# Constants for a hybrid GLA and RWKV-7 step: made on ScalarE at the start instead of on VectorE, with the planner's numbers set anew

## The chip, the cores and the metric

One core of one Trainium2 chip runs the kernel. The metric is the device time of one execution in microseconds (us). The engines are TensorE (PE in the profile; its weight loads are PEld), VectorE (DVE), ScalarE (ACT), GpSimd (POOL) and SyncE (SP), which issues all transfers.

## The reference

One layer of a decoder that has two parallel branches and a gated merge, for 1024 prompt tokens (they start from zero states) and 8 sample tokens (each with its own states). Everything is float32, the model is 1024 wide.

```python
p = x @ w_in                                    # 1024 -> 9360 columns
p_gla, p_rwkv, p_gate = split(p)
q, k, v, g_a, a_lr = split(p_gla)               # a_lr: 16 columns
log_a = log_sigmoid(a_lr @ gla_alpha_w2 + b) / 16
o_gla, S_gla = gla_chunked(q, k, v, log_a, S0)  # S_t = diag(a_t) S + k_t^T v_t ; o_t = q_t S_t
o_gla = rmsnorm(o_gla) * silu(g_a)
pr = p_rwkv + (prev - p_rwkv) * mu              # token shift
r, kb, vb, g_b, w_lr, aa_lr = split(pr)
...
y, S_rwkv = rwkv7_scan(r, w, k, v, kk, a, S0)   # S_t = S (diag(w) - kk^T (kk*a)) + v^T k ; y_t = S_t r_t
o_rwkv = (groupnorm(y) + bonus) * silu(g_b)
m = sigmoid(gate_a) * (o_gla @ w_up_gla) + sigmoid(gate_b) * (o_rwkv @ w_up_rwkv)
y_out = layernorm(2**0.25 * x + m @ w_out)
```

The outputs are `y_out` for both groups, the new states and the last projected row.

## The kernel before

Every large product is made of three TensorE passes on float32r parts: a value is split into a high part `hi` (a cast) and a low part `lo` (value minus high part), and `w_hi x_hi + w_hi x_lo + w_lo x_hi` is summed in PSUM. So ahead of the products stand, for each 128x520 block of x, a cast on ScalarE (`xh<-row`) and a subtraction on VectorE or GpSimd (`xl<-row,xh`), and for each 128x512 piece of weight a cast on ScalarE (`wpart<-wraw`) and a subtraction (`wpart<-wraw,wpart`). x lies in eight blocks of 128 rows (k = 0 to 7). The tokens go through in two passes: the first holds 512 prompt tokens and the 8 samples (tiles of 256 and 264 columns), the second 512 prompt tokens (one tile of 512).

The work is written as generators ("streams": blocks of the projection, GLA heads, pairs of RWKV heads, loads, gates). `Order.run` is a list scheduler that runs while the kernel is built. At each step it asks every stream for its next operation, estimates when that could start (`start`, from `self.time` of each engine, the time at which each tile is ready, and a table of hops between engines, `HOP`, with an extra `SPARE` where TensorE takes something from ScalarE, VectorE or GpSimd), subtracts the stream's precedence (`PRIO`, or `FOR_PE` for TensorE) and emits the best. The streams give the order on each engine; no engine leaves the order that was emitted. So a change of a number in these tables, or of any operation, can deal the whole order anew. `URGENT` is subtracted for the loads of weights and x while TensorE has no weight ready (`needed`). `SPARE_ROWS` and `EARLY_GATES` say how many row buffers stay free, and how many gates are loaded early, in `load_gates`.

What the start needs: `first_blocks` runs the first two blocks of the projection over the blocks of x as they arrive, with idle products (`pch<-warm`) between. `low_rank` makes the 16 columns of `a_lr` as a product of its own. Its weights stand in the constant `wa`, 66 columns wide for each k with the high part in columns 0 to 15, the low part in columns 32 to 47 and zeros between; its result goes into `alr`, of which rows 0 to 15, 32 to 47 and 64 to 79 are written and the others must be zero. `onesr` is a 128x128 matrix of ones. These three are float32r, and are written as copies of a float32 row: in `load_constants` VectorE sets a row to one, copies it into `onesr`, sets it to zero, and copies it into `alr` and `wa`. `load_constants` runs as a stream, so the scheduler places these five operations. `setup`, ahead of the scheduler, sets the tiles `XT` (two), `Yd` and `Xd` to zero on GpSimd.

In a GLA head (`gla_head`) each chunk of 128 tokens makes, in one PSUM bank, the output `po` (from the values and, but for the first chunk, from the state `S`), and the state's increment `pS` (in a trace `big<-row` 128x256). ScalarE copies `po` out in two pieces (`row<-big` 128x128), VectorE forms the next state (`S<-S,row,big`), and the next chunk's products (`big<-row,S`) take it. In the RWKV chain TensorE works through `pch` banks: `pch<-wide,gg`, `pch<-rh,XT` and `pch<-wide`, with a copy on ScalarE or a product on VectorE after each.

Of the kernel before, what the change touches and what calls it, by code (L numbers as in the profile page):

```python
# [14 lines left out]
AF = mybir.ActivationFunctionType  # L15
# [5 lines left out]
P = 128  # L21
D = 1024
NK = D // P
# [6 lines left out]
GH, GDK, GDV = 4, 128, 256  # L30
# [15 lines left out]
HALF = HT + NS  # L46
# [18 lines left out]
GROUP = 3  # L65
IDLE = 3
RANKW, RANKM = 48, 66
SPARE_ROWS = 11
EARLY_GATES = 13


HOP = {"P": 0.2, "D": 0.418, "G": 0.115, "V": 0.064, "A": 0.14}

SWITCH = 0.092
HOLD = 0.11
TABLE = 1.28

AGE = 1.045

SPARE = 0.411  # L80
LANDED = 0.648
BIAS = 0.193
ASIDE = 8.388

PRIO = {"evacuate": 0.39, "pair": 0.3, "turn": 0.5, "chain": 0.42, "norm": 0.1, "x": 0.61, "lora": 0.42, "rank":
        1.25, "head": 0.27, "gate": -0.38, "w": 0.3, "out": 0.04, "state": -0.13, "block": -0.38}
FOR_PE = {"pair": 1.0, "turn": 1.84, "chain": 0.8, "norm": 0.39, "lora": 0.29, "rank": 1.85, "head": 0.89, "gate":
        1.0, "state": 2.11, "out": 0.05}
STAND, SCARCE, PER_ROW = 0.034, 0.249, 0.148

URGENT = 1.707
SIGMOID, EXP = "sigmoid_and_others", "natural_log_exp_and_others"
SETS = {AF.Sigmoid: SIGMOID, AF.Tanh: SIGMOID, AF.Exp: EXP, AF.Ln: EXP}

# [165 lines left out]
class Order:  # L260
# [120 lines left out]
    def run(self):  # L381
        while self.streams:
# [48 lines left out]
class Kern(Order):  # L431
# [71 lines left out]
    def setup(self):  # L503
        nc, a = self.nc, self.a
# [18 lines left out]
        for k in range(NK):  # L523
            for v in "hl":
                tag = f"x{v}{k}"
# [47 lines left out]
        for tag, n, bufs in (("XT", 2 * HT, 2), ("Yd", HT, 1), ("Xd", HT, 1)):  # L573
            ts = [cp.tile([P, n], F32, name=f"{tag}{i}") for i in range(bufs)]
            for t in ts:
                nc.gpsimd.memset(t, 0.0)
            self.fixed(tag, ts)

    def load(self, name, op):

        if name in self.first:
            yield lambda: self.first[0] == name
        yield op
        if name in self.first:
            self.first.remove(name)

    def load_constants(self):
        a, V, E = self.a, self.V, self.E
        row, wa = yield from self.rows(2)
        wa = wa[:, :NK * 16]  # L590
        yield from self.load("pv", self.S.dma_start(self.pv, a["pv"]))
        yield from self.load("wa", self.S.dma_start(wa, a["wa"]))
        yield V.memset(row, 1.0)
        yield V.tensor_copy(self.onesr, row[:, :P])
        yield V.memset(row, 0.0)
        yield V.tensor_copy(self.alr, row[0:96])
        self.has.add("alr")
        yield V.tensor_copy(self.wa, row[:, :NK * RANKW + RANKM - RANKW])
        hi, lo = (self.wa[:, :NK * RANKW].rearrange("p (k c) -> p k c", c=RANKW)[:, :, o:o + 16] for o in (0, 32))
        wa3 = wa.rearrange("p (k c) -> p k c", c=16)  # L600
        yield V.tensor_copy(hi, wa3)
        yield V.tensor_sub(lo, wa3, hi.bitcast(F32))
        self.free(wa)
        self.has.add("wa")
        yield from self.load("shift", self.S.dma_start(self.shT, a["shiftT"]))
        o = PV["mu"][0]
        yield V.tensor_scalar(self.omu, self.pv[:, o:o + NRC], -1.0, 1.0, ALU.mult, ALU.add)
        o = PV["ka"][0]
        yield V.tensor_scalar(self.oka, self.pv[:, o:o + 8], -1.0, 1.0, ALU.mult, ALU.add)
        o = PV["kk"][0]  # L610
        yield V.tensor_scalar(self.nkk, self.pv[:, o:o + 8], -1.0, None, ALU.mult)
        self.has.add("pv")
        yield from self.load("cst", self.S.dma_start(self.cons, a["cst"]))
        raw, heads = row[0:96, :GH * GDK], (yield from self.row(P))
        yield self.S.dma_start(heads, a["heads"])
        for n in range(3):
            yield self.S.dma_start(raw[32 * n:32 * n + 16], a["gla_alpha_w2"])
        yield self.S.dma_start(self.lev, a["lev"])
        yield V.tensor_copy(self.gw2, raw)
        yield V.tensor_sub(self.gw2[64:96], raw[64:96], self.gw2[64:96].bitcast(F32))  # L620
        yield V.tensor_copy(self.headsr, heads)
        self.free(row, heads)
        self.has.add("cst")
# [176 lines left out]
    def low_rank(self, c, xs):  # L800

        yield lambda: len(xs) == NK and "wa" in self.has
        x_ = yield from self.row(c.n)
        for t0, n in c.tiles:
            q = yield from self.bank("big", [P, n])
            for k in range(NK):
                for v in range(2):
                    yield self.P.matmul(q[:RANKM], self.wa[:, RANKW * k:RANKW * k + RANKM], xs[k][v][:, t0:t0 + n],
                                        start=(k == v == 0), stop=(k == NK - 1 and v == 1))
            x = x_[0:16, t0:t0 + n]  # L810
            yield self.C.copy(x, q[0:16])
            yield self.V.tensor_add(x, x, q[32:48])
            self.free(q)

            hi, lo, hi2 = (self.alr[g:g + 16, t0:t0 + n] for g in (0, 32, 64))

            yield lambda: "alr" in self.has and (not c.i or self.decayed == GH)
            yield self.C.copy(hi, x)
            yield self.C.copy(hi2, x)
            yield self.V.tensor_sub(lo, x, hi.bitcast(F32))  # L820
            c.alr_ready += 1
        self.free(x_)
# [719 lines left out]
    def load_gates(self):  # L1542

        yield lambda: self.ctx[1].fronts >= NPAIR - 1
        for n in range(2):
            for c in self.ctx:
                for x in range(NK):
                    if x == EARLY_GATES:
                        yield lambda: self.ctx[1].fronts == NPAIR and self.ctx[1].gated == NPAIR + 2 * GH
                    gt = yield from self.row(c.n, SPARE_ROWS)  # L1550
                    yield self.S.dma_start(gt, self.sg[c.i][n][x])
                    m = None
                    if n:
                        m = yield from self.row(c.n, SPARE_ROWS)
                        yield lambda: c.half > x
# [302 lines left out]
```

## Time and profile before

| | |
|---|---|
| median of three runs | 1459.84 us (1459.55 to 1460.57) |
| the profiled execution's own time | 1459.23 us |
| its span, first to last instruction | 1457.3 us |
| TensorE busy | 1443.5 us, 99% of the span |
| VectorE, ScalarE, GpSimd busy | 1058.8, 828.9, 362.6 us |
| TensorE's granted clock, mean | 0.998 |

The profile shows one execution. The time of 1459.23 us lies 1.93 us above its span, and 0.61 us under the median of the runs. A row of a timeline gives the start in us from the span's start, the time it took, engine, line, operation, output and inputs, and in brackets how long the engine had been idle and what ended that. Nearly all rows have line 227, since the helper that records operations for the scheduler stands there, so rows are told apart by the names of their tiles.

### The profile page before, as it was taken

To read this page: it belongs to the slowest core of one execution; us is meant where nothing else is said; L and a number is where in the kernel's file an instruction comes from. 1 tells how busy PE (TensorE), PEld (TensorE's weight loads), DVE (VectorE), ACT (ScalarE), POOL (GpSimd) and SP (SyncE) were. 2 spreads that over 40 slices of the span, in tenths; PEclk is the share of its full clock that TensorE was granted. 3 is DMA by queue.
4 is the path that set the end of the run, shared out by engine and by line. 5 is a ranking of instruction groups with operands and counts; after the bars stand their busy time and mean duration, and the time that the engine had idled before them with its cause. 6 is when DMAs were issued, how large, how long until landed. Compare 5 with 4: busy or idle time off the path is not lost.

```text
span 1457.3 us, 30477 instructions
## 1 busy us (share of the span) xinstructions
PE 1443.5 (99%) x10768; PEld 1280.5 (88%) x10768; DVE 1058.8 (73%) x2208; ACT 828.9 (57%) x2114; POOL 362.6 (25%) x1111
## 2 busy tenths in 40 slices
PE   9999999999999999999999999999999999999997
PEld 8999999999999998878888888888788898898786
DVE  6687487958895889577747895787669856665665
ACT  5656667766776677455555565464557646643210
POOL 1060506050604160406051405411332330000000
PEclk9999999999999999999999999999999999999999
DMA  8786887678767885675466455746575768798432
GB/s 308 262 289 201 287 275 269 202 245 297 253 209 241 277 307 191 190 210 186 137 205 208 152 173 175 229 138 207 185 230 156 226 206 249 250 311 287 135 119 84
DMA packets 211315, 319.14 MB, mean 219 GB/s; under 512 B 91699, under 2 KB 107196, under 8 KB 211164
## 3 DMA queue, kind: packets, MB, share of 16 engines
q1 hardware_dynamic: 211164, 317.20, 67.6%
q8 instruction: 86, 1.41, 0.4%
q14 instruction: 65, 0.53, 0.1%
HBM read 197.45 MB, written 118.61 MB: 217 GB/s over the span
## 4 chain that ended last, share of the span: by engine, by line
PE 92%; DVE 3%; DMA 3%; ACT 1%; issue 1%; SPq 1%; DVEq 0%; ACTq 0%
PE proj L227 59%; PE big L227 27%; PE pch L227 6%; DVE row L227 1%; SPq L227 1%; DVE xl L227 0%; DMA wraw<-w_in 0%; DMA wide<-LD 0%; DVE wpart L227 0%; DMA row<-xT 0%; DMA wraw<-w_up_gla 0%; DMA row<-o_gla 0%; DMA wide<-Sp 0%; DVE XT L227 0%; DMA w<-wpart 0%
## 5 line engine op out<-in xcount | busy, mean ns | idle before, releaser
L227 PE MATMUL proj<-xh,wpart 128*128 128x264 f32 (+2 forms) x3696 | 901.3, 328 | 0.0
L227 PEld LDWEIGHTS proj<-xh,wpart 128*128 128x128 f32 x3696 | 614.2, 188 | 49.0 <-issue 6.5
L227 PE MATMUL proj<-xl,wpart 128*128 128x264 f32 (+2 forms) x1848 | 603.8, 327 | 0.0
L227 PEld LDWEIGHTS proj<-xl,wpart 128*128 128x128 f32 x1848 | 348.1, 188 | 23.6 <-issue 1.4
L227 POOL TENSOR_TENSOR Xt<-X,wide 128x60 f32<-128x60 f32 (+24 forms) x496 | 170.9, 344 | 676.5 <-DMA wide<-LD 281.4
L227 DVE TENSOR_TENSOR row<-row 128x256 f32<-128x256 f32 (+10 forms) x369 | 191.1, 530 | 14.6 <-ACT row L227 8.0
L227 DVE TENSOR_TENSOR wpart<-wraw,wpart 128x512 fp32r<-128x512 f32 x210 | 146.1, 698 | 74.4 <-ACT wpart L227 71.2
L227 ACT CAST wpart<-wraw 128x512 fp32r<-128x512 f32 x210 | 130.0, 621 | 100.1 <-PE proj L227 57.6
L227 POOL TENSOR_TENSOR X<-X,Xt 128x60 f32<-128x60 f32 (+24 forms) x496 | 170.3, 343 | 38.7
L227 ACT ACTIVATE row<-row 128x520 f32<-128x520 f32 (+4 forms) x229 | 137.7, 612 | 13.3 <-DMA row<-sg 5.6
L227 PE MATMUL big<-xh,wpart 128*128 128x256 f32 (+2 forms) x576 | 133.0, 320 | 0.2 <-DVE wpart L227 0.2
L227 PEld LDWEIGHTS big<-xh,wpart 128*128 128x128 f32 x576 | 95.3, 188 | 7.4 <-DVE wpart L227 0.4
L227 DVE TENSOR_TENSOR wide<-pch,gg 64x65 f32<-64x65 f32 x224 | 49.8, 222 | 65.1 <-PE pch L227 62.9
L227 ACT COPY row<-big 128x128 f32<-128x128 f32 (+6 forms) x152 | 49.7, 356 | 81.1 <-PE big L227 77.0
L227 PE MATMUL big<-xl,wpart 128*128 128x256 f32 (+2 forms) x288 | 92.2, 320 | 0.8 <-DVE xl L227 0.8
L227 DVE SCALAR_TENSOR_TENSOR row<-proj,pv,row 128x255 f32<-128x255 f32 (+1 forms) x95 | 54.6, 575 | 48.2 <-ACT tail L227 36.4
L227 ACT COPY rh<-pch 128x130 f32<-128x130 f32 x121 | 32.5, 268 | 98.8 <-PE pch L227 98.0
L227 ACT COPY wide<-pch 64x65 f32<-64x65 f32 x241 | 50.1, 208 | 50.4 <-PE pch L227 47.4
L227 ACT ACTIVATE row<-proj,omu 128x256 f32<-128x256 f32 (+1 forms) x95 | 52.2, 549 | 33.5 <-PE proj L227 32.5
L409 ACT ACT_TABLE_LOAD x54 | 69.3, 1283 | 0.9
L227 PE MATMUL big<-row 128*64 128x64 f32 (+4 forms) x648 | 65.0, 272 | 0.2 <-DVE gg L227 0.2
L227 PEld LDWEIGHTS big<-xl,wpart 128*128 128x128 f32 x288 | 54.2, 188 | 5.3 <-DVE xl L227 1.8
(234 smaller groups left out, 2069.6 us busy)
## 6 DMA issues: line engine op xcount, KB each, us to landing
w<-wpart SPq DMA_DIRECT2D x146, 512.0 KB, 4.3
wpart<-w SPq DMA_DIRECT2D x146, 512.0 KB, 3.8
wraw<-w_in SPq DMA_DIRECT2D x146, 256.0 KB, 4.2
wide<-LD SPq DMA_DIRECT2D x64, 128.0 KB, 3.8
wraw<-w_up_gla SPq DMA_DIRECT2D x32, 256.0 KB, 3.7
wraw<-w_up_rwkv SPq DMA_DIRECT2D x32, 256.0 KB, 3.7
sg<-row SPq DMA_DIRECT2D x16, 260.0 KB, 3.2
row<-sg SPq DMA_DIRECT2D x16, 260.0 KB, 4.3
```

Of the source, the lines that this page charges most:

```text
L227: ways.append((eng, lambda call=call: call(out, *args, **kw), price(eng, name, out, args, ins)))
L409: self.nc.scalar.preload_act_table_set(self.table)
```

## The change

The two copies into `wa` and `alr` and the ones of `onesr` move out of `load_constants` into `setup`: ScalarE makes them from the first `XT` tile, which GpSimd has just set to zero, ahead of everything that the scheduler emits (`onesr` as the zeros plus a bias of one). The scheduler then starts with ScalarE taken to 1.9 us and GpSimd to 2.1 us. VectorE loses five operations. A memset of the row that takes the low-rank weights of the heads (`raw`) stays, and goes to GpSimd. `low_rank` no longer waits for `alr`. The planner's numbers are changed in eleven places; the order is dealt anew from them.

```diff
-SPARE_ROWS = 11
-EARLY_GATES = 13
-HOP = {"P": 0.2, "D": 0.418, "G": 0.115, "V": 0.064, "A": 0.14}
-SWITCH = 0.092
+SPARE_ROWS = 12
+EARLY_GATES = 14
+HOP = {"P": 0.2, "D": 0.385, "G": 0.115, "V": 0.064, "A": 0.14}
+SWITCH = 0.114
...
-SPARE = 0.411
+SPARE = 0.232
...  # PRIO: "gate" -0.38 -> -0.04, "out" 0.04 -> -0.08; FOR_PE: "gate" 1.0 -> 0.91
-URGENT = 1.707
+URGENT = 2.228
...
             for t in ts:
                 nc.gpsimd.memset(t, 0.0)
+            if tag == "XT":
+                zero = ts[0]
+                nc.scalar.copy(self.wa, zero[:, :NK * RANKW + RANKM - RANKW])
+                nc.scalar.copy(self.alr, zero[0:96, :HALF])
+                nc.scalar.activation(self.onesr, zero[:, :P], AF.Identity, bias=self.bias["one"])
             self.fixed(tag, ts)
+        self.time["A"], self.time["G"] = 1.9, 2.1
...
-        yield V.memset(row, 1.0)
-        yield V.tensor_copy(self.onesr, row[:, :P])
-        yield V.memset(row, 0.0)
-        yield V.tensor_copy(self.alr, row[0:96])
-        self.has.add("alr")
-        yield V.tensor_copy(self.wa, row[:, :NK * RANKW + RANKM - RANKW])
...
         yield from self.load("cst", self.S.dma_start(self.cons, a["cst"]))
+        yield self.G.memset(row, 0.0)
...
-            yield lambda: "alr" in self.has and (not c.i or self.decayed == GH)
+            yield lambda: (not c.i or self.decayed == GH)
```

What it does to the order shows at three places. The first is VectorE at the start; the names `xl` and `xh` carry the number of their buffer, and `xl_264` before is `xl_268` now (k = 4). Before:

```order
L227 TENSOR_TENSOR xl_264<-row,xh_252 128x520
L227 MEMSET row 128x520
L227 TENSOR_TENSOR wpart<-wraw,wpart 128x512
L227 CAST onesr<-row 128x128
L227 MEMSET row 128x520
L227 TENSOR_TENSOR xl_299<-row,xh_263 128x520
L227 TENSOR_TENSOR xl_314<-row,xh_298 128x520
L227 TENSOR_TENSOR xl_324<-row,xh_313 128x520
L227 CAST alr<-row 96x520
L227 CAST wa<-row 128x402
L227 CAST wa<-row 128x8x16
L227 TENSOR_TENSOR wpart<-wraw,wpart 128x512
```

And now:

```order
L227 TENSOR_TENSOR xl_268<-row,xh_256 128x520
L227 TENSOR_TENSOR wpart<-wraw,wpart 128x512 x2
L227 TENSOR_TENSOR xl_303<-row,xh_267 128x520
L227 TENSOR_TENSOR xl_319<-row,xh_302 128x520
L227 TENSOR_TENSOR xl_332<-row,xh_318 128x520
L227 CAST wa<-row 128x8x16
L227 TENSOR_TENSOR wa<-row,wa 128x8x16
```

Five operations are gone between `xl` of k = 4 and the weights of `wa`, and the second weight subtraction, which stood behind `wa`, stands ahead of `xl` of k = 5.

The second is TensorE at the same place: k = 4 of the first two blocks, and the first product with `wa`. Before:

```order
L227 MATMUL big<-xh_252,wpart 128x264
L227 MATMUL big<-xh_252,wpart 128x256
L227 MATMUL big<-xl_264,wpart 128x256
L227 MATMUL big<-xh_200,wa 66x256
L227 MATMUL big<-xl_205,wa 66x256
```

And now:

```order
L227 MATMUL big<-xl_268,wpart 128x256
L227 MATMUL big<-xh_256,wpart 128x256
L227 MATMUL big<-xh_256,wpart 128x264
L227 MATMUL big<-xl_268,wpart 128x264
L227 MATMUL big<-xh_256,wpart 128x264
L227 MATMUL big<-xh_267,wpart 128x256
L227 MATMUL big<-xl_303,wpart 128x256
L227 MATMUL big<-xh_267,wpart 128x256
L227 MATMUL big<-xh_267,wpart 128x264
L227 MATMUL big<-xl_303,wpart 128x264
L227 MATMUL big<-xh_267,wpart 128x264
L227 MATMUL big<-xh_203,wa 66x256
```

The product with `wa` has moved behind ten more products, the rest of k = 4 and half of k = 5.

The third is the state of a GLA head in the first pass, on TensorE: the increment `pS` (128x256), and the next products that take the state formed from it. Before (`S_4694` is formed from bank `big_4666`):

```order
L227 MATMUL big_4666<-row_3423 128x256
L227 MATMUL pch_4661<-wide_2683,gg_2685 128x130
L227 MATMUL proj_4592<-xl6_314,wpart_4406 128x256
L227 MATMUL proj_4592<-xh6_298,wpart_4406 128x256
L227 MATMUL proj_4592<-xh7_313,wpart_4406 128x256
L227 MATMUL proj_4592<-xl7_324,wpart_4406 128x256
L227 MATMUL proj_4592<-xh7_313,wpart_4406 128x256
L227 MATMUL big_4696<-row_3424,row_3425 128x128
L227 MATMUL proj_4692<-xh0_200,wpart_4387 128x264
L227 MATMUL big_4696<-row_2610,S_4694 128x128
```

And now, in a chunk at about the same place of the program (`S_4543` is formed from `big_4514`):

```order
L227 MATMUL big_4514<-row_3382 128x256
L227 MATMUL pch_4524<-rh_4519,XT0_179 128x130
L227 MATMUL proj_4478<-xh4_256,wpart_4223 128x264
L227 MATMUL proj_4478<-xh5_267,wpart_4223 128x264
L227 MATMUL proj_4478<-xl5_303,wpart_4223 128x264
L227 MATMUL big_4545<-row_3383,row_3384 128x128
L227 MATMUL proj_4478<-xh5_267,wpart_4223 128x264
L227 MATMUL big_4545<-row_2713,S_4543 128x128
```

Between increment and use stand eight products before and six now. On ScalarE the two copies out of that bank, which VectorE's step waits for, and what stands between them, before:

```order
L227 COPY row_2870<-big_4666 128x128
L227 COPY rh_4683<-pch_4661 128x130
L227 ACTIVATE gg_2685<-wide_2683,pc_3031 128x130
L227 COPY row_2968<-big_4666 128x128
L227 ACTIVATE row_4591<-proj_4592,omu_89 128x256
```

And now:

```order
L227 COPY rh_4519<-pch_4498 128x130
L227 ACTIVATE gg_2617<-wide_2615,pc_2875 128x130
L227 COPY row_2898<-big_4514 128x128
L227 COPY wide_2615<-pch_4524 64x65 x2
L227 COPY row_2988<-big_4514 128x128
```

Two operations stand between the copies in both; `rh` and `gg` have moved ahead, two small copies out of `pch` have come in between. Over the whole program, of the 28 steps from an increment to the next use of the state, those with eight products or fewer between are three before (eight, seven and six of them) and six now (eight, eight, six, six, five and four).

More of the change, by code (lines that the diff above doesn't have):

```diff
@@ L85 @@
 PRIO = {"evacuate": 0.39, "pair": 0.3, "turn": 0.5, "chain": 0.42, "norm": 0.1, "x": 0.61, "lora": 0.42, "rank":
-        1.25, "head": 0.27, "gate": -0.38, "w": 0.3, "out": 0.04, "state": -0.13, "block": -0.38}
+        1.25, "head": 0.27, "gate": -0.04, "w": 0.3, "out": -0.08, "state": -0.13, "block": -0.38}
 FOR_PE = {"pair": 1.0, "turn": 1.84, "chain": 0.8, "norm": 0.39, "lora": 0.29, "rank": 1.85, "head": 0.89, "gate":
-        1.0, "state": 2.11, "out": 0.05}
+        0.91, "state": 2.11, "out": 0.05}
 STAND, SCARCE, PER_ROW = 0.034, 0.249, 0.148
-URGENT = 1.707
+URGENT = 2.228
 SIGMOID, EXP = "sigmoid_and_others", "natural_log_exp_and_others"
```

## The prediction

> **What bounds the kernel now.** I read the page first (busy time and the chain that ended last), then TensorE's waits, then the start by timelines, then the one place of the waits that the new order touches most.
>
> ```profile
> PE 1443.5 (99%) x10768; PEld 1280.5 (88%) x10768; DVE 1058.8 (73%) x2208; ACT 828.9 (57%) x2114; POOL 362.6 (25%) x1111
> PE 92%; DVE 3%; DMA 3%; ACT 1%; issue 1%; SPq 1%; DVEq 0%; ACTq 0%
> ```
>
> TensorE is busy in 1443.5 of the 1457.3 us of the span, and 92% of the chain is its work. The number of products does not change. So the time can only move through what TensorE stands idle, 13.8 us in all. The stretch after the last product is a part of that:
>
> ```profile
> 1449.80:1457.30 7.50, 0.00 (x0) 0.00 (x0) 4.38 (x9) 0.50 (x2) 0.00 (x0) 0.66 0.20 70
> ```
>
> The first number after a stretch is its length, then TensorE's busy time. The last 7.5 us hold no product, only the last layer norm and its store; the change does not touch it. That leaves 6.3 us, and the view of TensorE's waits names nearly all of it:
>
> ```profile
> PE big L227 <- DVE wa L227: 1.4, 1, 1.4
> PE pch L532 <- DVE warm L529: 1.1, 1, 1.1
> PE big L227 <- DVE gg L227: 0.9, 3, 0.3
> PE big L227 <- DVE xl L227: 0.8, 3, 0.4
> PE big L227 <- DVE S L227: 0.8, 2, 0.4
> PE big L227 <- DMA wraw<-w_up_gla: 0.4, 1, 0.4
> PE pch L227 <- DMA wide<-Sp: 0.4, 1, 0.4
> ```
>
> The columns are us in total, times, and the longest. The wait for `wa` is the longest single one; the warm-up (1.1) stays in any order. All others together are 3.8 us (0.2 each for `row` and `wpart` are left out here). 0.2% of the time, about what a measurement can tell from no change, is 2.9 us: more than the wait for `wa` and less than all that can be won.
>
> **The change part by part.** *The wait for `wa`.* TensorE's rows around it, and VectorE's:
>
> ```profile
> 13.78 0.41 PE L227 MATMUL big<-xh,wpart 128*128 128x264 f32 x2
> 14.02 0.28 PE L227 MATMUL big<-xl,wpart 128*128 128x256 f32 x1
> 15.71 0.33 PE L227 MATMUL big<-xh,wa 128*66 128x256 f32 x1 [1.41 <-DVE wa L227]
> 10.37 0.49 DVE L227 MEMSET row<- 128x520 f32 x1
> 10.78 0.63 DVE L227 TENSOR_TENSOR wpart<-wraw,wpart 128x512 fp32r<-128x512 f32 x1
> 11.33 0.21 DVE L227 CAST onesr<-row 128x128 fp32r<-128x128 f32 x1
> 11.72 0.49 DVE L227 MEMSET row<- 128x520 f32 x1 [0.17 <-DVE onesr L227]
> 12.12 1.85 DVE L227 TENSOR_TENSOR xl<-row,xh 128x520 fp32r<-128x520 f32 x3
> 13.89 0.42 DVE L227 CAST alr<-row 96x520 fp32r<-96x520 f32 x1
> 14.23 0.62 DVE L227 CAST wa<-row 128x402 fp32r<-128x402 f32 x2
> 14.77 0.68 DVE L227 TENSOR_TENSOR wpart<-wraw,wpart 128x512 fp32r<-128x512 f32 x1
> 15.37 0.28 DVE L227 TENSOR_TENSOR wa<-row,wa 128x128 fp32r<-128x128 f32 x1
> 9.75 1.29 ACT L227 CAST wpart<-wraw 128x512 fp32r<-128x512 f32 x2 [0.16 <-DMA wraw<-w_in]
> 11.10 2.01 ACT L227 CAST xh<-row 128x520 fp32r<-128x520 f32 x3
> ```
>
> TensorE starts one of these products every 0.12 us (13.78, then two products on, 14.02), and the one with `wa` starts 1.69 us after the one before it: 1.57 us lost. In the new order VectorE is free by 10.37. The two weight pieces are cast by 11.04, so both subtractions (0.68 each) end by 11.75; the three `xl` follow the casts of `xh`, the last of which ends at 13.11, and end by 13.8 at the latest (0.69 after). `wa` then takes the smaller of its two casts and the subtraction of 0.28, under 0.6 us together: ready by 14.4. TensorE has ten more products ahead of it, so it gets there at 14.02 + 11 x 0.12 = 15.34. Those ten find their weights (11.75) and `xl` of k = 5 (12.5). The margin is 0.9 us, and the 1.57 us go whole. What is late next is the second tile of the same product, which waits for the first one's sum to leave its bank; it waits 0.2 now and I leave it so.
>
> *The three operations on ScalarE.* Its start, and that of the first products:
>
> ```profile
> 0.74 1.28 ACT L527 ACT_TABLE_LOAD   x1 [0.74 <-PEq L1850]
> 3.56 0.63 ACT L227 CAST xh<-row 128x520 fp32r<-128x520 f32 x1 [1.53 <-DMA row<-xT]
> 6.07 0.62 ACT L227 CAST xh<-row 128x520 fp32r<-128x520 f32 x1 [1.27 <-DMA row<-xT]
> 7.48 0.39 PE L227 MATMUL big<-xl,wpart 128*128 128x256 f32 x1 [0.35 <-DVE xl L227]
> L576 POOL MEMSET XT<- x2: 952/952/952, 0.7 to 1.6; 128x1024 f32 x2
> ```
>
> ScalarE sits idle from 2.02 to 3.56, and `XT` is zero at 0.74 + 0.95 = 1.69. A cast of 520 columns takes 0.63 and one of 512 takes 0.62 (4.18 in the same row of casts above is 0.62 after 3.56), so `alr` costs 0.63, `wa` (402 columns) some 0.5, and `onesr` (128 columns, a form not in the trace) between 0.2, VectorE's cast of that size, and 0.5. From 2.02 that ends at 3.35 to 3.68: the first `xh` is late by at most 0.12. That is hidden: the second `xh` waits for its transfer until 6.07, and TensorE waits for what comes of it at 7.48, so a start 0.12 later only shortens that wait of 0.35. Cost nothing; with the cover gone it would be 0.12.
>
> The Trainium skill (ScalarE: Activation LUTs, What ACT_TABLE_LOAD costs) gives 186 ns plus 0.833 ns a column, 93 more with a bias from memory, and an overlap of 93 between neighbours: by it an estimate of 1.34 us for the three, which would end at 3.36; the casts here (0.63 for 520) agree with its 0.62. The Trainium skill (Perfetto Trace Analysis, Optimizing Scalar/DVE Operations) speaks against such a move, since VectorE is faster where it has a performance mode: the 0.42 for `alr` on VectorE against 0.63 on ScalarE bears that out, and by it the sum would lose up to 0.2 us an operation, if ScalarE were not idle there.
>
> *GpSimd's memset of the row for the low-rank weights* stands behind the memsets of the start and is used by transfers that go out after 16 us; it costs nothing, and if it did, the wait would be for the decay of the first head, tens of us later.
>
> *The new numbers.* `SPARE` falls from 0.411 to 0.232 us: the scheduler believes that TensorE can take a result 0.18 us sooner, and puts its products that much closer behind the work that feeds them. Where the old order left a margin this costs nothing, where it had none it is a stall. The GLA state is where I can price it:
>
> ```profile
> 297.81 0.59 PE L227 MATMUL big<-row 128*128 128x256 f32 x2
> 298.24 0.39 PE L227 MATMUL pch<-wide,gg 128*128 128x130 f32 x2
> 298.44 0.27 ACT L227 COPY row<-big 128x128 f32<-128x128 f32 x1 [0.86 <-PE big L227]
> 298.66 0.27 ACT L227 COPY rh<-pch 128x130 f32<-128x130 f32 x1
> 298.82 0.41 ACT L227 ACTIVATE gg<-wide,pc 128x130 f32<-128x130 f32 x1
> 299.13 0.26 ACT L227 COPY row<-big 128x128 f32<-128x128 f32 x1
> 299.42 0.48 DVE L227 SCALAR_TENSOR_TENSOR S<-S,row,big 128x256 f32<-128x256 f32 x1 [1.06 <-ACT row L227]
> 299.95 0.50 PE L227 MATMUL big<-row,S 128*128 128x128 f32 x2 [0.40 <-DVE S L227]
> L227 ACT COPY wide<-pch 64x65 f32<-64x65 f32 x241 | 50.1, 208 | 50.4 <-PE pch L227 47.4
> ```
>
> The increment leaves TensorE at 298.40. VectorE's step waits for the second copy on ScalarE, held up by `rh` and `gg` between, and TensorE starts again at 299.95, 1.55 us after the increment and 0.40 late. In the new order two small copies (0.21 each by the last row, a group of the page) stand between instead: copies at 0.04, 0.22, 0.34 and 0.5 after the increment, its end at 0.75, VectorE 0.78 to 1.26, TensorE at about 1.3. But TensorE gets there sooner: the chain product (0.22), three products (0.36), 0.22 and 0.12 from 298.24 on would be 0.76 after the increment. So it stalls for 0.5 us, and at the other three tight places (six, five and four products between) for 0.4 to 0.5: 4 x 0.5 = 2.0 against the 0.8 of now, so 1.2 us more. From below it is 0 (ScalarE finishes sooner than I think), from above 4 x 0.9 - 0.8 = 2.8, if a delay like that of 298.66 to 299.13 comes in as well.
>
> All other waits (3.0 us without the state) are dealt anew; I take them as they are, between 0 and twice that.
>
> The sum: -1.57 + 1.2 = -0.4 against the profiled execution's 1459.23, which gives 1458.9, and 1459.5 against the median of the runs, which lies 0.6 above that execution. I say **1459.4**.
>
> **The rivals.** *Faster.* The tight places cost nothing, since ScalarE and VectorE come in time, and the other waits fall by half in an order that was dealt with more urgency for loads: -1.57 - 0.4 - 1.5 = -3.5, that is 1456.0, halfway between the two ways of counting as in the sum. For it: 5.1 us of TensorE's idle time are open to any order, and most hand-overs cost nothing even now. Against it: nothing in the diff aims at `gg`, `xl` or the two transfers in the list of waits.
>
> *Slower: the margin of 0.18 us was needed.* The rows of the RWKV chain say how much hangs on it:
>
> ```profile
> L227 PE MATMUL pch<-wide,gg 128*128 128x130 f32 x256 | 50.1, 277 | 0.4 <-DMA wide<-Sp 0.4
> L227 PE MATMUL pch<-wide 128*128 128x130 f32 x256 | 49.7, 276 | 0.0
> ```
>
> The last columns are the count, the time, and the idle time ahead. Each product is two rows, so with the one with `rh` that stands between these two the chain has 3 x 128 = 384 hand-overs, and next to no idle time ahead of them (0.0, and 0.4 for a transfer). If one in ten loses 0.15 us, that is 5.8 us: -1.57 + 5.8 = +4.2, or 1463.7 in the same way. It decides from 4.5 us of new waits on, 12 ns a hand-over on average. For it: the order does stand tighter. Against it: the idle of 0.0 us shows a margin well kept now, but not how much of it is spare.
>
> *The wait for `wa` stays*, because TensorE waits there for something else (a weight's transfer, a bank): no gain, and the 1.2 us remain, 1460.4 to 1461.0. Against it: every input of the ten products is ready by 12.5 in the rows above.
>
> **How the numbers follow.** The forecast has 0.47, the wait that stays 0.05, the faster case 0.25, the slower one 0.23. The forecast and the wait that stays lie within 0.2% (1456.9 to 1462.8): same 0.52. The range reaches to the other cases from both sides and leaves about a tenth out on each: from 1456.0 (all of the gain at `wa`, no tight place, some more) to 1463.8 (the hand-overs at one in ten). The likeliest case by itself is 1457.9 (no stall at the states) to 1461.1 (all of 2.8).
>
> **What would show it.** Right: no idle time of TensorE before the first `big<-xh,wa`, which starts at about 15.3; ScalarE's three operations between 2.0 and 3.7 us; `DVE S` in TensorE's waits at some 2 us in four or more pieces; the first real product at the same 4.9 us. Wrong: the list of waits without `DVE S` (the price of the new numbers fails), or `ACT wide`, `ACT rh` and `DVE wide` in it with several us (the slower rival), or the wait at `wa` under another name. A changed busy time of TensorE of more than a few us would show that the number of changes of product shape, which I take as no cost, matters.

## The result and the profile after

| | before | after |
|---|---|---|
| median, runs on the same chip | 1459.69 us (4 runs) | 1469.76 us (4 runs, 1467.72 to 1473.34) |
| ratio, 95% interval | | 1.0072 (1.0060 to 1.0084) |
| the profiled execution, its span | 1459.23, 1457.3 us | 1467.72, 1465.9 us |

The changed kernel is 0.7% slower. That is outside the predicted range (1456.0 to 1463.8), on the side to which the prediction gave 0.23. The page of after, busy time and the chain that ended last:

```profile
PE 1450.4 (99%) x10768; PEld 1278.8 (87%) x10768; DVE 1061.0 (72%) x2217; ACT 834.3 (57%) x2108; POOL 360.2 (25%) x1111
PE 89%; DVE 6%; DMA 2%; ACT 1%; issue 1%; SPq 0%; POOL 0%; DVEq 0%; POOLq 0%; ACTq 0%
```

The count of products is the same, 10768, yet TensorE is "busy" for 6.9 us more (1443.5 before). The busy time of its weight loads (PEld) went down a little, from 1280.5. VectorE's share of the chain doubled.

The start went as the change says. ScalarE and TensorE of after:

```profile
2.03 0.53 ACT L579 CAST wa<-XT 128x402 fp32r<-128x402 f32 x1
2.47 0.62 ACT L580 CAST alr<-XT 96x520 fp32r<-96x520 f32 x1
2.99 0.40 ACT L581 ACTIVATE onesr<-XT,b_one 128x128 fp32r<-128x128 f32 x1
3.49 0.62 ACT L227 CAST xh<-row 128x520 fp32r<-128x520 f32 x1
4.82 0.39 PE L227 MATMUL big<-xh,wpart 128*128 128x256 f32 x1
14.83 0.28 PE L227 MATMUL big<-xh,wpart 128*128 128x264 f32 x1
14.95 0.28 PE L227 MATMUL big<-xh,wa 128*66 128x256 f32 x1
```

ScalarE's three operations lie between 2.03 and 3.39 us, the first `xh` is not late (3.49, 3.56 before), the first product starts at 4.82, and the first product with `wa` follows its neighbour by 0.12 us, without a wait. So the ten microseconds were lost behind that. TensorE's waits of after (us in total, times, longest):

```profile
PE big L227 <- DVE S L227: 2.0, 3, 0.7
PE pch L532 <- DVE b_one L542: 1.1, 1, 1.1
PE pch L227 <- DVE wide L227: 0.9, 3, 0.5
PE pch L227 <- POOL wide L227: 0.9, 1, 0.9
PE big L227 <- DVE xl L227: 0.8, 4, 0.2
PE big L227 <- DVE gg L227: 0.6, 3, 0.2
PE big L227 <- ACT xh L227: 0.6, 1, 0.6
```

This list explains almost nothing: with its two shorter rows it comes to 7.3 us, and to 6.2 before. The answer stands in the same view of the weight loads (PEld), whose rows name late inputs that the products' rows leave out. The rows that are compared below, before:

```profile
PEld big L227 <- DVE gg L227: 2.2, 5, 0.6
PEld big L227 <- DVE xl L227: 1.8, 4, 0.6
PEld big L227 <- DVE wa L227: 1.6, 1, 1.6
PEld big L227 <- DVE part L227: 1.4, 3, 0.9
PEld big L227 <- DVE S L227: 1.3, 2, 0.7
PEld pch L227 <- PE proj L227: 0.3, 1, 0.3
```

After:

```profile
PEld big L227 <- DVE xl L227: 4.1, 12, 0.6
PEld big L227 <- DVE S L227: 3.6, 6, 0.9
PEld pch L227 <- PE proj L227: 3.1, 7, 0.9
PEld big L227 <- DVE part L227: 2.5, 8, 0.6
PEld big L227 <- ACT Xt L227: 1.7, 5, 0.4
PEld big L227 <- DVE gg L227: 1.2, 3, 0.4
PEld pch L227 <- POOL wide L227: 1.1, 1, 1.1
```

All rows of this view that name a cause sum to 15.4 us in 32 pieces (single waits) before and 26.9 us in 69 pieces after. (Rows marked "issue", idle time for which the profile shows no cause, are left out: 21.4 before, 21.5 after.) The difference is 11.5 us, while the span grew by 8.6: part of a load's wait lies beside a product that still runs. No single piece of after is longer than 1.1 us. The releaser in a row is not always the cause. Where loads of the chain name "PE proj", the product itself names VectorE's `wide`, which is what it takes:

```profile
376.86 0.46 PE L227 MATMUL pch<-wide,gg 128*128 128x130 f32 x2 [0.24 <-DVE wide L227]
376.83 0.30 PEld L227 LDWEIGHTS pch<-wide,gg 128*128 128x128 f32 x2 [0.41 <-PE proj L227]
```

By stretches of the span, in us and pieces:

| | 0 to 20 | 20 to 400 | 400 to 800 | 800 to 1150 | 1150 to 1340 |
|---|---|---|---|---|---|
| before | 3.6 / 4 | 3.7 / 7 | 3.5 / 9 | 2.5 / 7 | 2.3 / 5 |
| after | 1.7 / 3 | 5.8 / 12 | 7.0 / 18 | 7.3 / 21 | 5.4 / 15 |

Why the products' own view misses them shows where the second stage of projections (the merge) begins. TensorE's products and weight loads of after, and VectorE:

```profile
1160.13 0.40 PE L227 MATMUL big<-xh,wpart 128*128 128x256 f32 x2
1160.49 0.39 PE L227 MATMUL big<-xl,wpart 128*128 128x256 f32 x1
1160.71 0.40 PE L227 MATMUL big<-xh,wpart 128*128 128x256 f32 x2
1161.20 0.38 PE L227 MATMUL big<-xl,wpart 128*128 128x256 f32 x1
1160.49 0.19 PEld L227 LDWEIGHTS big<-xl,wpart 128*128 128x128 f32 x1 [0.17 <-DVE xl L227]
1161.20 0.19 PEld L227 LDWEIGHTS big<-xl,wpart 128*128 128x128 f32 x1 [0.30 <-DVE xl L227]
1159.63 3.03 DVE L227 TENSOR_TENSOR xl<-row,xh 128x520 fp32r<-128x520 f32 x4 [0.75 <-ACT xh L227]
```

A block of x gives three products of 0.12 us, while VectorE needs 0.7 us for the block's `xl`. TensorE therefore waits at both blocks shown (1160.49, 1161.20). The products' rows name no idle time there. In a stream a product is drawn 0.28 us long although the next one starts 0.12 later (14.83 and 14.95 above), so its row can cover some 0.16 us of a hole behind it; and the two that waited are themselves drawn 0.38 and 0.39 long. The loads' rows show the waits, 0.17 and 0.30. The Trainium skill (Perfetto Trace Analysis, Identifying the Most-Contended Engine) says that the busy share of matmuls is not a good measure of how close TensorE is to its peak, and names the busy share of the weight loads as one to use instead. This trace agrees: the one time rose by 6.9 us with the same products, the other didn't.

### The profile page after: what moved, and what is told of

It is laid out like the page before. It is cut to its first block, busy times and chain, and to the rows that moved or that the text cites. A ratio compares the mean times of both kernels' runs of the same rounds, so it can differ in the third digit from the quotient of the medians.

```text
span 1465.9 us, 30466 instructions
## 1 busy us (share of the span) xinstructions
PE 1450.4 (99%) x10768; PEld 1278.8 (87%) x10768; DVE 1061.0 (72%) x2217; ACT 834.3 (57%) x2108; POOL 360.2 (25%) x1111
## 4 chain that ended last, share of the span: by engine, by line
PE 89%; DVE 6%; DMA 2%; ACT 1%; issue 1%; SPq 0%; POOL 0%; DVEq 0%; POOLq 0%; ACTq 0%
PE proj L227 57%; PE big L227 27%; PE pch L227 6%; DVE row L227 2%; DVE wpart L227 1%; DVE wide L227 1%; DMA wraw<-w_up_gla 0%; ACT xh L227 0%; ACT row L227 0%; DVE part L227 0%; DVE gg L227 0%; DMA row<-o_rwkv 0%; DMA row<-o_gla 0%; DVE xl L227 0%; SPq L227 0%
## 5 line engine op out<-in xcount | busy, mean ns | idle before, releaser
L227 PE MATMUL proj<-xh,wpart 128*128 128x512 f32 (+2 forms) x3696 | 902.8, 329 | 0.0
L227 PE MATMUL proj<-xl,wpart 128*128 128x512 f32 (+2 forms) x1848 | 605.9, 328 | 0.0
L227 POOL TENSOR_TENSOR Xt<-X,wide 128x60 f32<-128x60 f32 (+24 forms) x496 | 163.5, 330 | 673.2 <-DMA wide<-LD 306.2
L227 DVE TENSOR_TENSOR row<-row 128x256 f32<-128x256 f32 (+9 forms) x369 | 189.7, 529 | 7.8 <-ACT row L227 1.6
L227 POOL TENSOR_TENSOR X<-X,Xt 128x60 f32<-128x60 f32 (+24 forms) x496 | 175.2, 353 | 38.7
L227 ACT COPY row<-big 128x128 f32<-128x128 f32 (+7 forms) x146 | 49.4, 364 | 91.7 <-PE big L227 86.5
L227 PE MATMUL big<-row 128*64 128x64 f32 (+5 forms) x652 | 65.9, 273 | 0.2 <-DVE gg L227 0.2
```

What stands on the lines that cost most here:

```text
L227: ways.append((eng, lambda call=call: call(out, *args, **kw), price(eng, name, out, args, ins)))
```

## Experiments

Three theories stood against one another: the move itself costs something; the smaller `SPARE` costs it (the prediction's slower rival, here "margin"); or any order that is dealt anew is worse than the old one ("deal"). The first four runs set parts of the change against one another.

**The move alone, in the old order.** The old code makes the constants on ScalarE, and the scheduler still counts the four removed operations, so that TensorE's order is the old one in every position:

```diff
+def ghost(op):
+    op.ways = [(eng, lambda: None, cost) for eng, _, cost in op.ways]
+    return op
...  # setup as in the change
-        yield V.tensor_copy(self.onesr, row[:, :P])
+        yield ghost(V.tensor_copy(self.onesr, row[:, :P]))
...  # the first memset and the copies into alr and wa likewise
```

> The kernel before, with the constants made on ScalarE at the start; the scheduler still counts the four operations that VectorE no longer does (one memset of the row stays), so the order of every other operation is the old one, word for word. Both theories (the margin theory: the smaller SPARE makes the stalls; the deal theory: any order dealt anew makes them, the old one being a lucky one) expect the wait for wa to fall and nothing else to move: 0.8 to 1.6 us less than before, so 1458.1 to 1458.9 against 1459.7. If the move itself were to blame, it would be slower than before.

1457.86 us against 1460.03: ratio 0.9987 (0.9978 to 0.9996). TensorE at the place:

```profile
14.62 0.33 PE L227 MATMUL big<-xh,wa 128*66 128x256 f32 x1 [0.37 <-DVE wa L227]
```

The product with `wa` starts 1.09 us sooner than the 15.71 of before, with 0.37 us of the wait left. So the move isn't what costs. The gain of 2.2 us in the medians is a little more than the 0.8 to 1.6 expected, and about twice what this place explains; a run further down tests it again.

**The numbers alone.** The old code with all eleven new numbers (the order is that of after but for 85 positions in the first 45 us):

```diff
-SPARE = 0.411
+SPARE = 0.232
...  # and the other ten
```

> The kernel before with the new numbers; the constants stay on VectorE. TensorE's order is that of the changed kernel but for 85 places in the first 45 us. Margin theory and deal theory: as slow as the changed kernel and 1.6 us more, 1469 to 1472. If the move is to blame: about 1459.7.

1472.48 us: ratio 1.0091 (1.0072 to 1.0111), half a microsecond above the range expected. That is 12.4 us over before, while after, which has the move as well, is 10.1 over its own; the intervals of the two ratios overlap, so the difference isn't shown to be the move. The loss belongs to the order that the numbers deal.

**The new code with the old numbers.**

```diff
-SPARE = 0.232
+SPARE = 0.411
...  # and the other ten back
```

> The changed kernel with all numbers of before. Margin theory: 1457 to 1460, since SPARE is 0.411 again. Deal theory: the order is a new one, picked by nobody, so slower than before: 1463 to 1475. In this order 25 hand-overs from ScalarE or VectorE to TensorE stand closer than the shortest such hand-over in the trace of before, by 16 us in sum, which speaks for the second.

1497.72 us: ratio 1.0259 (1.0244 to 1.0275). The largest loss of the four, with none of the new numbers, and far above the ranges of both theories (1457 to 1460, 1463 to 1475). TensorE late in it:

```profile
1271.58 0.46 PE L227 MATMUL pch<-wide,gg 128*128 128x130 f32 x2 [0.97 <-DVE wide L227]
1272.40 0.65 PE L227 MATMUL pch<-rh,XT 128*128 128x130 f32 x2 [0.36 <-ACT rh L227]
1273.62 0.80 PE L227 MATMUL pch<-wide 128*128 128x130 f32 x2 [0.57 <-ACT wide L227]
1275.06 0.77 PE L227 MATMUL pch<-wide,gg 128*128 128x130 f32 x2 [0.64 <-DVE wide L227]
```

The RWKV chain runs alone here: no product of the projection is left to fill the time of its hand-overs, so every hand-over is idle time, 0.36 to 0.97 us each. In this order the chain's last product starts at 1294 us, before at 1254 and after at 1245.

**After with the old margin alone.**

```diff
-SPARE = 0.232
+SPARE = 0.411
```

> The changed kernel with one number back: SPARE 0.411 instead of 0.232. Margin theory: the stalls at hand-overs go, 1457 to 1461. Deal theory: one more new order, as slow as any, 1463 to 1475. In this order 3 hand-overs stand closer than the shortest of before, by 0.4 us in sum (9 and 1.8 us in the changed kernel).

1496.01 us: ratio 1.0245 (1.0228 to 1.0262), again above both ranges. The time is 26 us above that of after. But the profile splits it: between 20 and 1150 us the named waits of the loads fall from 20.1 to 11.6 us, and most of what is lost is lost at two places behind that:

```profile
1284.85 0.34 PE L227 MATMUL big<-cons,row 64*128 64x64 f32 x1 [18.10 <-DMA row<-w_out]
1291.07 0.58 PE L227 MATMUL proj<-xh,wpart 128*128 128x256 f32 x1 [4.99 <-ACT xh L227]
```

So undoing one number can't be read off in the time, as the rest of the order changes with it. The next runs therefore vary numbers that mean nothing, to see what a new order costs by itself.

**The margin alone, and three nudges.** The old code with `SPARE` 0.232; the old code with `BIAS`, and with `STAND`, moved in the third decimal; after with that `STAND`:

```diff
-SPARE = 0.411
+SPARE = 0.232
```

> The old code and all the old numbers but one: SPARE is 0.232 instead of 0.411; the order of TensorE differs from the old one in 5550 of 9093 positions. Margin theory (the smaller margin makes many small waits, whatever else is dealt): the waits of TensorE's weight loads with a named cause rise from the 15.4 us of the old kernel by 8 to 14 us, as they rose to 26.9 in the changed kernel, with at least twice the old 33 pieces, and the time is about as much longer: 1466 to 1476. Deal theory (any order dealt anew loses, at a few places that chance sets): the number of pieces stays near 33 and the loss, if large, is in one to three places of over 1 us each; a time anywhere from 1462 to 1500.

```diff
-BIAS = 0.193
+BIAS = 0.194
```

> The old code and numbers, but BIAS, a small preference between ScalarE and VectorE, is 0.194 instead of 0.193; TensorE's order is the old one up to its position 5221 of 9093 and differs in 2049 positions behind that. SPARE is the old one, so the margin theory expects the named waits of the weight loads within 3 us of the old 15.4 and a time of 1458 to 1463. Deal theory: even this loses 5 to 40 us, all of it behind position 5221 (past 800 us), in a few large places.

```diff
-STAND, SCARCE, PER_ROW = 0.034, 0.249, 0.148
+STAND, SCARCE, PER_ROW = 0.035, 0.249, 0.148
```

> The old code and numbers, but STAND, a weight on TensorE's precedences, is 0.035 instead of 0.034; TensorE's order differs in 5610 positions, from position 965 on. SPARE is the old one. Margin theory: 1458 to 1463, as few pieces of waits as in the old kernel (33). Deal theory: slower by 5 to 40 us. Counted from this order and the durations in the old trace, 15 hand-overs of it are shorter than any seen in the old trace, by 8 us together, so the deal theory says at least 1467.

```diff
 SPARE = 0.232
...
-STAND, SCARCE, PER_ROW = 0.034, 0.249, 0.148
+STAND, SCARCE, PER_ROW = 0.035, 0.249, 0.148
```

> The changed kernel with STAND 0.035 instead of 0.034: its order differs from the changed kernel's in 5988 positions, with the same SPARE of 0.232. Margin theory: about the changed kernel's time, 1466 to 1474, with the same many small waits (33 to 70 pieces, 22 to 30 us named at the weight loads). Deal theory: another draw, anywhere from 1462 to 1500, and not near the changed kernel's.

The margin alone took 1485.99 us (1.0182, 1.0165 to 1.0198), the nudge of `BIAS` 1471.52 (1.0081, 1.0059 to 1.0103), that of `STAND` 1501.29 (1.0285, 1.0266 to 1.0305), and after with the nudge 1489.07 (1.0208, 1.0191 to 1.0225). The three nudges have no purpose, and they cost 12, 42 and 19 us (the last against after). All four times lie above the margin theory's ranges (1466 to 1476 for the margin alone, 1458 to 1463 for the first two nudges, 1466 to 1474 for the last), and in the deal theory's, but for the nudge of `STAND`, which passes its 40 us by 2. So the margin theory is refuted as an account of the time. The pieces fit neither theory. With the margin alone the loads have 30.6 us of named waits in 62 pieces, more time than the margin theory said and nearly its number of pieces, where the deal theory had them stay near 33; with the nudge of `STAND` there are 60 pieces with the old margin. Some pieces are large, each from its own place: those of 0.9 us or more in TensorE's waits, without those at the start, come to 6 of the 11 us by which the profiled span is longer with the nudge of `BIAS`, 16 of 39 with that of `STAND`, and 18 of 20 in after with it. The longest of each:

```profile
1052.94 0.60 PE L227 MATMUL proj<-xh,wpart 128*128 128x512 f32 x1 [2.92 <-DMA wpart<-w]
```

```profile
1170.50 0.79 PE L227 MATMUL big<-part,headsr 128*128 128x512 f32 x1 [10.21 <-ACT part L227]
```

```profile
1282.55 0.58 PE L227 MATMUL big<-xh,wpart 128*128 128x256 f32 x1 [10.31 <-ACT xh L227]
```

**Dose of the margin.** What was left of the margin theory was the long stretch from 20 to 1150 us. The two-part theory says that `SPARE` sets the many small waits there, and that chance sets those around the merge. So `SPARE` was set to two more values in the old code.

```diff
-SPARE = 0.411
+SPARE = 0.05
```

> The old code and numbers with SPARE 0.05. Read from the runs so far: between 20 and 1150 us the waits of the weight loads with a named cause are 9.4 to 15.9 us (21 to 33 pieces) in the six orders with SPARE 0.411, and 15.8 to 20.9 us (39 to 51 pieces) in the four with 0.232, while the stretch from 1150 to 1340 us holds anything from 2 to 33 us in both groups. Two-part theory (SPARE sets the many small waits of the long steady stretch in any order; the stretch around the merge is dealt by chance): 25 us or more in 65 pieces or more between 20 and 1150 us. Deal theory alone (the two groups differ by chance): 9 to 21 us, as in the others. The time follows from no theory to better than 1470 to 1510.

```diff
-SPARE = 0.411
+SPARE = 0.6
```

> The old code and numbers with SPARE 0.6. Two-part theory: the named waits of the weight loads between 20 and 1150 us are as low as with 0.411 or lower, at most 11 us in at most 25 pieces; what the time is depends on the stretch from 1150 to 1340 us, where a step of the RWKV chain that comes later still leaves TensorE without other work: 1458 to 1505. Deal theory alone: 9 to 21 us between 20 and 1150 us.

1482.13 us (1.0155, 1.0136 to 1.0173) and 1500.39 us (1.0280, 1.0254 to 1.0306). Between 20 and 1150 us the low one has 23.4 us in 65 pieces: as many pieces as the two-part theory asked for, a little less time than its 25. The high one has 16.4 us in 28 pieces, against at most 11 in 25: a miss. In the low one the RWKV chain's hand-overs lead the list of that stretch:

```profile
PEld pch L227 <- PE proj L227: 4.5, 13, 0.5
PEld big L227 <- DVE part L227: 3.2, 8, 0.9
PEld big L227 <- DVE l2p L227: 2.6, 8, 0.6
PEld big L227 <- ACT Xt L227: 2.4, 7, 0.4
```

**The whole code change in the old order.** As in the move alone, and the memset of the row goes to GpSimd:

```diff
+        zero = V.memset(row, 0.0)
+        zero.ways = [(eng, lambda: self.nc.gpsimd.memset(row, 0.0), cost) for eng, _, cost in zero.ways]
+        yield zero
```

> The code change whole, in the old order: the four operations go to ScalarE as in the change, the memset of the row for the heads' low-rank weights goes to GpSimd (in the run with the move alone it stayed on VectorE), old numbers, and the scheduler still counts the removed operations, so that the order of TensorE is the old one in all 9093 positions. In the run with the move alone 0.37 us of the wait for wa were left, behind VectorE's memset of 0.49 us. Theory: that goes too, so 1.6 us less than the old kernel in all: 1457.5 to 1458.5, against 1457.9 with the move alone. Rival (the move itself costs something, at the start or on GpSimd): not faster than the old kernel.

1458.72 us, 12 runs against 17 of before with 1459.35: ratio 0.9999 (0.9991 to 1.0008), no difference that can be measured. TensorE and VectorE at the place:

```profile
14.80 0.34 PE L227 MATMUL big<-xh,wa 128*66 128x256 f32 x1 [0.37 <-DVE wa L227]
13.72 0.22 DVE L227 CAST wa<-row 128x128 fp32r<-128x128 f32 x1
13.86 0.68 DVE L227 TENSOR_TENSOR wpart<-wraw,wpart 128x512 fp32r<-128x512 f32 x1
14.46 0.29 DVE L227 TENSOR_TENSOR wa<-row,wa 128x128 fp32r<-128x128 f32 x1
```

The 1457.5 to 1458.5 us expected were missed. The same 0.37 us are left, so VectorE's memset was not what held `wa`: in the old order a weight subtraction of 0.68 us stands between its cast and its subtraction. The product starts 0.91 us sooner than before. Of this gain the two runs give 0.6 and 2.2 us in the medians; which of them is nearer to the truth can't be told, and at this place no more than 0.9 to 1.1 is seen in the traces. What both show is that the move, in the old order, doesn't cost the ten microseconds.

**A late change of order alone.** Two runs keep TensorE's old order up to 1162 and 1128 us. The first has two of the changed numbers, the second a nudge:

```diff
-SPARE_ROWS = 11
-EARLY_GATES = 13
+SPARE_ROWS = 12
+EARLY_GATES = 14
```

> The old code and numbers with SPARE_ROWS 12 and EARLY_GATES 14, two of the changed numbers. The order of TensorE is the old one up to position 7435 of 9093, that is up to 1162 us, and differs in 389 positions behind it. Theory that the stretch around the merge is dealt by chance: up to 1150 us the waits are the old kernel's (10 us, 23 pieces, within 3 us); between 1150 and 1340 us they may be anything between the old kernel's 2 us and 33 us, and the time is 1459 plus what they are over 2 us. Rival (a late change of order costs nothing much, and it was what came before that made the large losses of the other orders): within 2 us of 2 us there, and a time of 1458 to 1462.

```diff
-"gate": -0.38   # PRIO
+"gate": -0.37
```

> The old code and numbers with one precedence of the gates at -0.37 instead of -0.38 (the change sets it to -0.04). The order of TensorE is the old one up to position 7258, that is up to 1128 us, and differs in 658 positions behind it. The theories expect of it what they expect of the run with the rows and gates: by the theory of chance the time is 1459 plus what the waits between 1150 and 1340 us are over 2 us, anything up to 30 us; by the rival 1458 to 1462.

1464.34 us (1.0029, 1.0012 to 1.0046; one of its five runs took 4995.21 us, which I can't explain) and 1462.50 us (1.0017, 1.0007 to 1.0027). The waits between 1150 and 1340 us are 8.0 us in the first, for which the theory of chance gives 1465; the rival, with 1458 to 1462 and at most 4 us of waits, missed. They are 2.6 in the second, as the rival has it; there the theory of chance gives 1459.6 and missed by 3 us, and the rival missed by half a microsecond. That run lost 1.0 us at a state of a GLA head at 1130 us. Both are slower, by 5 and 3 us, so these two late changes brought no loss of 20 to 40 us. The traces show that the change isn't quite so late on the other engines: in the first run ScalarE's order differs from 1098 us on, and 1.2 of the 8.0 us are a wait for ScalarE at 1155.76, ahead of TensorE's first change; in the second SyncE issues its transfers in another order from 907 us on.

**All orders side by side.** Named waits of the weight loads, us and pieces, from the profile of each:

| kernel | `SPARE` | time less before, us | 20 to 1150 us | 1150 to 1340 us |
|---|---|---|---|---|
| before | 0.411 | | 9.7 / 23 | 2.3 / 5 |
| the move alone, old order | 0.411 | -2.2 | 11.9 / 25 | 2.4 / 4 |
| whole code change, old order | 0.411 | -0.6 | 10.4 / 25 | 2.8 / 7 |
| nudge of the gates | 0.411 | 3.2 | 11.7 / 26 | 2.6 / 6 |
| rows and gates | 0.411 | 5.1 | 11.8 / 25 | 8.0 / 14 |
| nudge of `BIAS` | 0.411 | 12.0 | 15.9 / 33 | 2.3 / 5 |
| after with the old margin | 0.411 | 36.0 | 11.6 / 30 | 13.6 / 15 |
| new code, old numbers | 0.411 | 37.7 | 9.4 / 21 | 23.0 / 33 |
| nudge of `STAND` | 0.411 | 41.7 | 9.6 / 25 | 33.3 / 32 |
| after | 0.232 | 10.1 | 20.1 / 51 | 5.4 / 15 |
| the numbers alone | 0.232 | 12.4 | 20.9 / 50 | 3.8 / 11 |
| the margin alone | 0.232 | 26.4 | 15.8 / 39 | 12.1 / 20 |
| after with the nudge | 0.232 | 29.5 | 19.3 / 42 | 17.2 / 12 |
| the lowest margin | 0.05 | 22.8 | 23.4 / 65 | 5.5 / 11 |
| the highest margin | 0.6 | 41.0 | 16.4 / 28 | 16.5 / 7 |

(The columns don't hold all of the loss. After 1340 us the highest margin has another 9.7 us in 5 pieces, no other more than 1.7. Waits marked "issue" at the loads are left out: 39.5 us in "after with the old margin", among them the 18 us for the transfer of `w_out`; 31.9 in the new code with the old numbers, 30.3 with the lowest margin, 20.6 to 27.2 in the others.) The first three rows have TensorE in one and the same order, and so show the scatter from run to run: 9.7 to 11.9 us in 23 to 25 pieces in the long stretch. Two things are read from the table. Every one of the twelve orders that differ from the old one is slower than it, by 3 to 42 us, whatever was changed. And the pieces of the long stretch follow `SPARE`: 21 to 33 with 0.411, 39 to 51 with 0.232, 65 with 0.05. With 0.6 there are 28, and more time than the fewer pieces would say, so more margin than the old one buys nothing further.

## Why the prediction was wrong, step by step

**What held.** The wait for `wa` went whole, as the term of -1.57 us has it: the first product with `wa` starts at 14.95 us without idle time (15.3 was said). ScalarE's three operations are hidden; the Trainium skill (ScalarE: Activation LUTs, What ACT_TABLE_LOAD costs) gave an estimate of 1.34 us for them, and 2.03 to 3.39 is 1.36. GpSimd's memset costs nothing that a run shows. The stalls at the GLA states come to the price in TensorE's waits, 2.0 us against 0.8, which is the +1.2 of the sum, but partly by luck: they are three of 0.66 to 0.68 us in place of four of 0.5. At the one at 287.89 us ScalarE's second copy ends 1.03 us after the increment, where the prediction, which had counted the copies closer to one another, put 0.75. After loses 2.4 us less than the numbers alone do, which has the sign of the move's term but isn't clear of the noise.

**The step that failed** is "All other waits (3.0 us without the state) are dealt anew; I take them as they are, between 0 and twice that". It failed in its size and in its value.

Its size was read from the wrong view. In the products' rows the term even looks right, 3.0 us before and 7.3 - 1.1 - 2.0 = 4.2 after, inside its bounds; but of the 8.6 us by which the span grew, 6.9 are in what those rows draw as busy. The sentence "So the time can only move through what TensorE stands idle, 13.8 us in all" takes that busy time for work. By the weight loads, the waits besides `wa`, the warm-up and the state were 15.4 - 1.6 - 1.1 - 1.3 = 11.4 us before, nearly four times the 3.0. In after they are 26.9 - 1.1 - 3.6 = 22.2 us. So they did rise to twice what they were, the upper bound that the prediction set, but from 11.4 and not from 3.0: +10.8 us in the loads' rows. With -1.6 for `wa` and +2.3 for the state at the loads, this is the 11.5 us by which the named waits grew. The prediction's bound by itself allowed no more than +3.0.

Its value, "as they are", takes the old order for an ordinary one. It isn't: each of the twelve other orders that were run takes longer. The nudges show this without any theory of what a number does. That the old numbers were tuned until their order was a good one would explain it, but no run here shows how they were found.

Two smaller slips don't bear on the outcome. The faster rival takes off 0.4 us for the states where the rows have 0.8, and the upper end of the likeliest case, 1461.1, is counted on the median alone (1460.8 in the way of the other sums).

**The slower rival** had a part of the mechanism, but put all of it in one place. It forecast 5.8 us over 38 hand-overs of the RWKV chain. The chain's named waits at the loads rose from 1.0 us in 3 pieces to 5.4 in 12 up to 1150 us; the rest came as `xl` at the blocks of x (+2.3), `S` (+2.3), `part` (+1.1), `Xt` (+1.7) and others. That `SPARE` is behind the number of these pieces is supported by the groups of the table and by after with the old margin, in which they fall back to 30. It is not proved: in every run the order changed as well, the groups nearly touch, and 0.6 breaks the series. That `SPARE` explains the time is refuted: with the old one the time is anything from 1462.5 to 1501 us.

**What stays open** is why the long losses around the merge come about in one order and not in another. The traces show three ways: the RWKV chain's last product comes late (at 1290 and 1294 us in two of the three worst with the old margin) and the chain runs alone; or it ends in time and TensorE runs out of products before `o_rwkv` or `w_out` has come back from memory; or, as at 1170.50 with the nudge of `STAND`, TensorE stands for 10 us behind a long run of VectorE's operations ahead of `part`. The two late changes brought none of them about. No run isolates what earlier decision does.

The prediction's last sign, that a changed busy time of TensorE would show that changes of product shape matter, was a wrong reading too: the busy time changed by 6.9 us while the loads' named waits rose by 11.5, so hidden waits are enough to explain it. That changes of shape have no share at all isn't shown: counted with the usual distance of each pair of products in the old trace, the new sequence comes out between 4 us shorter and 2 us longer, depending on the way of counting.

## What to carry to other kernels

Where a scheduler deals the order from a table of numbers, test a code change with the order held (let the scheduler go on counting what was removed); otherwise its gain of 1 us drowns in a new order, which here cost 3 to 42 us. Before a sum is made of TensorE's waits, read the waits of its weight loads too: the products' rows showed 6.2 of 15.4 us before and 7.3 of 26.9 after. Give the forecast of a re-dealt order the spread of a few meaningless nudges, not the waits of the old order: none of twelve new orders was faster here.

## What the hardware showed beyond that

TensorE's granted clock fell where it was starved in small pieces. In the new code with the old numbers the columns behind TensorE's, VectorE's, ScalarE's and GpSimd's busy times are the granted clock, the share of the transfers' engines and GB/s:

```profile
1270.00:1274.00 4.00, 1.98 (x8) 1.33 (x8) 3.82 (x9) 1.46 (x6) 0.00 (x0) 0.82 0.85 271
1274.00:1280.00 6.00, 3.57 (x10) 2.12 (x9) 2.19 (x10) 4.97 (x12) 0.00 (x0) 0.50 0.38 116
1290.00:1300.00 10.00, 7.80 (x77) 6.12 (x76) 2.84 (x8) 5.19 (x13) 0.00 (x0) 0.50 0.76 218
```

No idle time of TensorE in that stretch is longer than 1.0 us (1.14 by the loads), yet the granted clock is 0.50 from 1274 us on and still so up to 1300. The pair of products `pch<-wide,gg` takes 0.77 us at 1275.06 where it took 0.46 at 1271.58. A round of the chain's three products, from one `pch<-rh,XT` to the next, took 3.42 us at 1268.98 and takes 3.95 at 1276.19: the round was long before the clock fell, and the lower clock adds half a microsecond. It also slows what follows the chain, up to 1300 us. The Trainium skill (TensorE: Matmul & The Clock Gate, A second HAM failure mode: psum-queue depth-cycling) tells of short idle times between groups of products that make the clock swing between the half and the full one. This trace agrees in that the clock fell to half behind short idle times; it shows no swing, since the clock stays at 0.50 for the rest of the chain. The mean clock of that run's neighbours in the table is lower too (0.987 with the nudge of `STAND` and with the old margin put back), that of after and before is 0.999 and 0.998.
